# A hybrid decoder step on one core: scheduler priority for the attention's maxima and exponentials, other banks behind the decode's small products, and the closing steps moved

## The chip, the core and the metric

The program runs on one core of one Trainium2 chip. Five engines work side by side: TensorE (PE in the profile, its weight loads PEld), VectorE (DVE), ScalarE (ACT), GpSimd (POOL) and SyncE (SP). Each has a queue of its own, whose order the program fixes; SP and POOL issue most of the DMA transfers. TensorE's products go to PSUM, of which this kernel uses eight banks of 128 x 512 float32. The metric is device time in microseconds (us) of one launch; the verdict compares medians.

## The reference

One decoder layer is computed twice with the same weights: for a prompt of 1024 rows and for eight sample sequences with one new row each, which attend to 8192 cached positions in pages. Per layer: an input projection; eight heads of forgetting attention (softmax with a cumulated log gate) beside eight heads of spatial gating, both normalized and projected out; cross-attention to 256 memory tokens; a gated MLP with a short convolution. The part that this case touches is the attention of the prompt and the softmax of the samples:

```python
def fox_attend(q, k, v, cq, ck, qpos, kpos):
    s = jnp.einsum('bqhd,bkhd->bhqk', q, k).astype(jnp.float32) * (ATT_HEAD_DIM ** -0.5)
    s = s + (cq.astype(jnp.float32).transpose(0, 2, 1)[:, :, :, None]
             - ck.astype(jnp.float32).transpose(0, 2, 1)[:, :, None, :])
    s = jnp.where(kpos[None, :] <= qpos[:, None], s, -jnp.inf)
    p = jax.nn.softmax(s, axis=-1).astype(v.dtype)
    return jnp.einsum('bhqk,bkhd->bqhd', p, v)
```

```python
def merge_heads(att, sgu, g_att_out, g_sgu_out, w_o):
    return jnp.concatenate([rmsnorm(att, g_att_out), rmsnorm(sgu, g_sgu_out)], axis=-1) @ w_o
```

## The kernel before

**Two streams in one program.** `prompt()` (L1843) is a Python generator that traces the prompt's work: the input projections, the attention of the first 512 rows (`attention(0)`, mixed with the memory projections and the first half of the gating), the attention of the second 512 rows (`attention(1)`), and then, for each half, output projection, cross-attention and MLP. Each `yield t` states roughly how much work was traced. `sample()` is a second generator with the samples' work; a driver loop takes one step of it whenever the yields have added up to the pace of the phase (`PACE`, L76). So the samples' instructions lie between those of the prompt in program order.

**Who orders the queues.** A scheduler reads the traced program and fixes the order of each engine's queue when the program is built: among the instructions that are ready in its own model of time it takes the one with the highest priority, which is program order, earlier first. `tc.high_priority()` lifts the instructions of a block ahead of others that are ready. `tc.issue_after(x)` puts the block's instructions on the engine of `x` behind `x` in that queue; it adds an order and no wait. On the chip the order is fixed; each instruction waits only for its data and its buffers.

**The attention.** For each pair of heads (`hp`, four of them), each block of 256 rows (`blk`, two), each head `j` and each tile of 128 rows `ii`, `scores` (L795) writes one tile of scores with three matmuls per chunk (two where the chunk is off the diagonal): L807, L809 and, on the diagonal, the mask L811. In the first half a tile has one chunk in one bank `ba`; in the second it has two chunks in a pair of `ba` banks, of which there are two pairs. VectorE takes the negated maximum of each row (L813, L816), ScalarE the exponential with its row sums (L814, L817) into `p_`. `turn` (L829) transposes `p_` on TensorE (L836), up to four tiles of 128 x 128 per bank, and copies them to `u` or `t2` tiles on ScalarE (L843) or, for every fourth bank of the second half, on VectorE (L841). `values` (L845) multiplies with V (L852) and evicts (L861); `back` (L866) transposes the result (L872) and scales it (L874). `turn`, `values` and `back` go through a queue that lags two score tiles behind (`LA`). `setup` (L743) prepares the next pair of heads: transposes of q and k, copies, low parts (L774, L788) and loads (L759, L769 to L771).

**Banks.** `ba` has four banks, `bb` two, and one each is tagged `ms` and `dv`. The transposes, the values and the results of the attention take `bb`, and every third time `ms` (`B3`, L825, with `M3 = 3`). The memory projections and others take `ba`, and every third time `bb` (`BK`, L146).

**The decode of the samples.** For each of eight sequences and 16 steps, `kstep` (L1416) gathers 1 MB of cached K by an indirect DMA on the POOL queue (L1419) into one of four `kv` buffers; VectorE multiplies by q and sums. In the attention phases a step is cut into four pieces of a product (L1426) and a sum (L1427); elsewhere the pieces are larger (L1435, L1439). `vstep` (L1478) gathers V likewise (L1481) and TensorE multiplies it with the weights into `dv` (L1487). Between them stand three small products, each in the bank `ms` with one VectorE reader: `gates` (L1402: product L1409, read by L1411), `soft_all` (L1456: transpose L1459, read by L1462) and `soft_exp` (L1468: product L1472, read by L1474). `vmask` (L1498) reads `dv`.

**Closing a half.** `close` (L947) takes the squares of the attention's rows on ScalarE (`ssq_into`, L230), the reciprocal root, scales the rows in place on VectorE (L958) and stores them to DRAM (`an_d`, L960, on SP); it is a generator of three steps. In `prompt()` the first step of `close(0)`, the squares, is traced before `attention(1)`; `beside` (L963) then lets `attention(1)` run and takes one step of the closing after its yields number 0 and 2. The two first yields of `attention(1)`, which set up its first pair of heads, have been taken earlier, so number 0 is the one after its first tile of scores. `merge_in` (L981) reads the stored rows back. `lastexp` holds the exponential that was traced last.

Of the kernel before, what the change touches and what calls it, by code (L numbers as in the profile page):

```python
# [78 lines left out]
def build(nc, tc, ctx, a, phases=None):  # L79
# [61 lines left out]
    def BB():  # L141
        return psum.tile([P, 512], F32, tag="bb", bufs=2 + MB, name=nm("bb"))
# [8 lines left out]

    def MS():
        return BB() if MB else psum.tile([P, 512], F32, tag="ms", bufs=1, name=nm("ms"))

    def DV():
        return psum.tile([P, 512], F32, tag="dv", bufs=1, name=nm("dv"))
# [569 lines left out]
    def attention(hf, late=None, at=3):  # L726
# [68 lines left out]
        def scores(qkv, ls, blk, j, ii):  # L795

            qab, ka, kb, _ = qkv
            i = blk * 2 + ii
            e = (hf * 4 + i + 1) * P
            nch = 1 if e <= 512 else 2  # L800
            n = e // nch
            p_ = (WRAW(e) if PW else U([P, e])) if hf else T2(e)
            mx = sm([P, 1], "mx", 4)
            both = BA2().rearrange("p (c n) -> p c n", c=2)[:, :, :n] if nch == 2 else BA()[:, :n].unsqueeze(1)
            for ch in range(nch):
                s = both[:, ch, :]
                mmul(s, qab[j][:, 0, i * P : (i + 1) * P], ka[j][:, ch * n : ch * n + n], start=True, stop=False)  # L807
                diag = ch == nch - 1
                mmul(s, qab[j][0:68, 1, i * P : (i + 1) * P], kb[j][0:68, ch * n : ch * n + n], start=False, stop=not diag)  # L809
                if diag:  # L810
                    mmul(s[:, n - P :], ident_b, cmask_b, start=False, stop=True)  # L811
            if nch == 1:
                nc.vector.tensor_reduce(mx, s, axis=AX.X, op=ALU.max, negate=True)  # L813
                nc.scalar.activation(p_[:, :e], s, AF.Exp, bias=mx, accum_out=ls[:, ii, j : j + 1])  # L814
            else:
                nc.vector.tensor_reduce(mx, both, axis=AX.XY, op=ALU.max, negate=True)  # L816
                nc.scalar.activation(  # L817
                    p_[:, :e].rearrange("p (c n) -> p c n", c=2), both, AF.Exp, bias=mx, accum_out=ls[:, ii, j : j + 1]
                )
            lastexp[:] = [newest(ENG.Activation)]  # L820
            return p_

# [1 line left out]

        def B3():  # L825
            turns[1] += 1
            return MS() if turns[1] % M3 == M3 - 1 else BB()

        def turn(p_, pts, n, ii):  # L829

# [116 lines left out]
    def close(hf, att):  # L947

        ssa = sm([P, 4], "ssa", 1)
        for i in range(4):  # L950
            ssq_into(ssa[:, i : i + 1], att[i // 2][:, i % 2, :])
        yield
        r = rstd_of(ssa, AW, 4, "ra")
        yield
        for b2 in range(2):
            for i in range(2):
                t = att[b2][:, i, :]
                nc.vector.tensor_scalar(t, t, r[:, b2 * 2 + i : b2 * 2 + i + 1], None, op0=ALU.mult)  # L958
            t0 = hf * 4 + b2 * 2
            nc.sync.dma_start(an_d[t0 * P : (t0 + 2) * P, :].rearrange("(c p) d -> p c d", p=P), att[b2])  # L960
        yield
# [403 lines left out]
    def decode():  # L1365
# [36 lines left out]
        def gates(b, A):  # L1402
# [1 line left out]
            nc.vector.tensor_tensor(  # L1404
                tot, A.rearrange("p (h k) -> p h k", k=64)[:, :, 63], lfz[:, b * 8 : b * 8 + 8], op=ALU.add
            )
            ps = MS()
            with behind(ENG.PE):
                mmul(ps[:, :8], suf, tot, start=True, stop=True)  # L1409
            dt_ = dec("dec").rearrange("p (k h) -> p k h", h=8)  # L1410
# [43 lines left out]
            return pm  # L1454

        def soft_all(b, pm):  # L1456
            ps = MS()
            with behind(ENG.PE):
                nc.tensor.transpose(ps[:8, :P], pm, ident)  # L1459
            with tc.high_priority():  # L1460
# [6 lines left out]

        def soft_exp(b, st, dg):  # L1468
            s = st[1]
            ps = MS()  # L1470
            with behind(ENG.PE):
                mmul(ps[:, :8], ones, dg, start=True, stop=True)  # L1472
            with tc.high_priority():
# [369 lines left out]
    def prompt():  # L1843
# [24 lines left out]
        if LT > 3:  # L1868
            yield next(att1)
        ending = close(0, att)  # L1870
        next(ending)
        phase[0] = "att1"
        ba_pool(True)
        if G0R:
            att = yield from mix(gating(0), att1, 1 / G0R)
        else:
            att = yield from beside(att1, ending, (0, 2))
        ba_pool(False)
        ending = close(1, att)
        next(ending)  # L1880
# [143 lines left out]
```

## Time and profile before

| | |
|---|---|
| median of 3 runs | 1807.73 us (1807.55 to 1808.47) |
| profiled execution, its time | 1812.65 us |
| profiled execution, span from first to last instruction | 1810.9 us |
| mean granted TensorE clock of it | 0.987 |
| first attention half, beside the memory projections | about 262 to 374 us |
| second attention half | about 374 to 503 us |
| output projection and cross-attention, first half | about 503 to 724 us |
| first MLP | about 724 to 1098 us |

The profile shows one execution. Busy time counts an engine's instructions and no register, branch, semaphore or DMA-issuing ones; matmuls are pipelined, so their durations overlap. A wait is named by the instruction that waited and the one whose end released it. The granted clock is the share of the full TensorE clock that was passed in a stretch. A row of a timeline gives start, duration, engine, line, operation, output <- inputs, shapes and count, and in brackets the idle time of the engine before it with its releaser.

### The profile page before, as it was taken

The numbers are of one execution on the slowest core, as the hardware profiler recorded it, in microseconds if no ns is written. First come the engines' busy times: TensorE is split into PE (matmuls) and PEld (weight loads), VectorE is DVE, ScalarE is ACT, GpSimd is POOL, SyncE is SP. The second block draws the span as 40 slices with busy tenths as digits, with TensorE's granted clock in tenths as the row PEclk, the third lists the DMA queues.
The fourth block names the chain that finished last, engine by engine and source line by source line (L and its number), as shares of the span: only waits on it lengthen the run. The fifth ranks groups of instructions, "written<-read, shape, count | busy, mean of one in ns | idle before, by whom it ended". The sixth has DMA issues, their size and how long they took to land.

```text
span 1810.9 us, 25097 instructions
## 1 busy us (share of the span) xinstructions
PE 1741.1 (96%) x9637; PEld 1295.4 (72%) x9637; DVE 1398.3 (77%) x1729; ACT 735.3 (41%) x1378; POOL 503.7 (28%) x461
## 2 busy tenths in 40 slices
PE   8999999878999899999999999999989999999997
PEld 5887776656677667777777777766676678767775
DVE  4689668987788887999999899888875549855344
ACT  6332265465633544433323244235353323232332
POOL 1252333522133323233232132433322111001110
PEclk9999999988999999999999999999999999999999
DMA  8886889786596876689788788979878677568982
GB/s 300 305 296 228 303 303 341 251 276 195 214 403 259 344 306 269 261 285 342 298 293 320 291 310 309 382 286 361 315 273 318 241 278 263 182 262 292 360 313 82
DMA packets 157074, 521.06 MB, mean 288 GB/s; under 512 B 20874, under 2 KB 40842, under 8 KB 124186
## 3 DMA queue, kind: packets, MB, share of 16 engines
q0 software_dynamic: 57168, 341.14, 49.7%
q1 hardware_dynamic: 92874, 165.73, 26.5%
q10 hardware_dynamic: 6912, 12.59, 1.8%
q8 instruction: 76, 1.25, 0.3%
q14 instruction: 44, 0.36, 0.1%
HBM read 495.47 MB, written 23.93 MB: 287 GB/s over the span
## 4 chain that ended last, share of the span: by engine, by line
PE 50%; issue 8%; DMA 8%; DVE 7%; POOL 2%; ACT 1%; POOLq 0%; DVEq 0%; ACTq 0%
PE ba L272 6%; PE ba L274 6%; PE ba L273 6%; DMA kv<-cache_v,io 6%; PE dv L1487 3%; PE bb L272 3%; PE bb L273 3%; PE bb L274 3%; DVE s L1439 1%; DVE kv L1435 1%; DVE wl L236 1%; PE dv L331 1%; DMA kv<-cache_k,io 1%; PE dv L1763 1%; POOL kv L1419 1%
## 5 line engine op out<-in xcount | busy, mean ns | idle before, releaser
L235 ACT ACTIVATE wh<-wr 128x1024 fp32r<-128x1024 f32 (+2 forms) x220 | 228.2, 1043 | 451.2 <-PE ba L273 143.2
L236 DVE TENSOR_TENSOR wl<-wr,wh 128x1024 fp32r<-128x1024 f32 (+2 forms) x220 | 263.1, 1202 | 173.8 <-PE ba L274 57.1
L1419 POOL DMA_INDIRECT kv<-cache_k,io x128 | 196.7, 1537 | 578.5 <-DVE s L1439 323.1
L1435 DVE TENSOR_TENSOR kv<-kv,d 128x1024 f32<-128x1024 f32 (+1 forms) x156 | 258.1, 1682 | 32.6 <-DMA kv<-cache_k,io 27.3
L1439 DVE TENSOR_REDUCE s<-kv 128x16 f32<-128x1024 f32 (+1 forms) x156 | 258.6, 1676 | 0.0
L1481 POOL DMA_INDIRECT kv<-cache_v,io x128 | 167.6, 1310 | 258.7 <-PE dv L1487 179.9
L273 PE MATMUL ba<-u,wh 128*128 128x512 f32 x528 | 208.5, 395 | 2.4 <-DVE u L239 2.4
L272 PE MATMUL ba<-u,wh 128*128 128x512 f32 x528 | 209.5, 397 | 0.0
L274 PE MATMUL ba<-u,wl 128*128 128x512 f32 x528 | 209.1, 396 | 0.0
L272 PE MATMUL ba<-wh,u 128*128 128x512 f32 (+1 forms) x495 | 186.1, 379 | 0.9 <-ACT u L235 0.9
L273 PE MATMUL ba<-wl,u 128*128 128x512 f32 (+1 forms) x495 | 185.2, 375 | 1.3 <-DVE wl L236 1.3
L274 PE MATMUL ba<-wh,u 128*128 128x512 f32 (+1 forms) x495 | 183.4, 375 | 0.0
L1487 PE MATMUL dv<-kv,s 128*32 128x512 f32 x1024 | 123.9, 598 | 4.8 <-DMA kv<-cache_v,io 4.8
L274 PEld LDWEIGHTS ba<-u,wl 128*128 128x128 f32 x528 | 99.2, 188 | 29.1 <-issue 5.7
L273 PEld LDWEIGHTS ba<-u,wh 128*128 128x128 f32 x528 | 99.3, 188 | 27.0 <-DVE u L239 2.6
L272 PEld LDWEIGHTS ba<-u,wh 128*128 128x128 f32 x528 | 99.5, 189 | 25.7 <-issue 4.0
L272 PEld LDWEIGHTS ba<-wh,u 128*128 128x128 f32 x495 | 93.0, 188 | 25.0 <-issue 6.5
L272 PE MATMUL bb<-u,wh 128*128 128x512 f32 x272 | 108.5, 399 | 0.0
L273 PE MATMUL bb<-u,wh 128*128 128x512 f32 x272 | 108.0, 397 | 0.0
L274 PE MATMUL bb<-u,wl 128*128 128x512 f32 x272 | 107.9, 397 | 0.0
L273 PEld LDWEIGHTS ba<-wl,u 128*128 128x128 f32 x495 | 93.0, 188 | 20.3 <-DVE wl L236 2.1
L274 PEld LDWEIGHTS ba<-wh,u 128*128 128x128 f32 x495 | 92.9, 188 | 19.4 <-issue 1.6
(444 smaller groups left out, 3330.5 us busy)
## 6 DMA issues: line engine op xcount, KB each, us to landing
wr<-w_up SPq DMA_DIRECT2D x88, 512.0 KB
kv<-w_up POOLq DMA_DIRECT2D x22, 1024.0 KB
wr<-w_down SPq DMA_DIRECT2D x40, 512.0 KB
kv<-w_down POOLq DMA_DIRECT2D x11, 1024.0 KB
wr<-w_in SPq DMA_DIRECT2D x16, 512.0 KB
wr<-w_o SPq DMA_DIRECT2D x16, 512.0 KB
wr<-w_cq SPq DMA_DIRECT2D x16, 512.0 KB
wr<-w_co SPq DMA_DIRECT2D x16, 512.0 KB
```

Of the source, the lines that this page charges most:

```text
L235: nc.scalar.activation(h, src, AF.Copy)
L236: nc.vector.tensor_tensor(l, src, h.bitcast(F32), op=ALU.subtract)
L272: mmul(out, sh, mh, start=(i == 0), stop=False)
L273: mmul(out, sh, ml, start=False, stop=False)
L274: mmul(out, sl, mh, start=False, stop=(i == n - 1))
L331: mmul(ps[32 * j : 32 * j + 32, :w], xT[:, k, :] if nk == 8 else xT[:, k * 8 : k * 8 + 32], raw[:, q, j * w : (j + 1) * w], start=(k == 0) ...
L1419: nc.gpsimd.indirect_dma_start(kv, None, a["cache_k"], off(kidx[:, b, ch : ch + 1]))
L1435: nc.vector.tensor_tensor(kvv[:, i : i + m, :], kvv[:, i : i + m, :], qb.unsqueeze(1).broadcast_to((P, m, 512)), op=ALU.mult)
L1439: nc.vector.tensor_reduce(s[:, ch * 4 + i : ch * 4 + i + m, :].rearrange("p k h -> p (k h)"), kvv[:, i : i + m, :].rearrange("p k (h d) -> ...
L1481: nc.gpsimd.indirect_dma_start(kv, None, a["cache_v"], off(kidx[:, b, ch : ch + 1]))
L1487: mmul(dv[32 * j : 32 * j + 32, :], s[:, ch * 4 : ch * 4 + 4, :].rearrange("p k h -> p (k h)"), kvv[:, j, :], start=(ch == 1), stop=(ch == ...
L1763: mmul(ps[32 * j : 32 * j + 32, :P], xsT[:, k, :], rvs[j // 2][:, k, j % 2, :], start=(k == 0), stop=(k == 7), tile_position=(0, 32 * j),)
```

## The change

Four edits. A new function `MSD` gives the same `ms` bank as `MS` and sets a counter to 2; the three small products of the decode use it. `B3`, at the turns at which it would give `ms`, looks at the counter: while it is above 0 it counts down and gives `bb`. The maximum and the exponential of `scores` are traced under `tc.high_priority()`. The squares of `close` are queued behind the exponential that was traced last. And the first step of `close(0)` isn't taken before `attention(1)` but at the yield number 0 within it, the second at number 2 and the third at number 4, so that the squares follow the first tile of scores, the reciprocal root the third, and scaling and store the first half of the next pair's set-up, which comes after the fourth.

```diff
+    small_ = [0]
+
+    def MSD():
+        small_[0] = 2
+        return MS()
...
-            if nch == 1:
-                nc.vector.tensor_reduce(mx, s, axis=AX.X, op=ALU.max, negate=True)
-                nc.scalar.activation(p_[:, :e], s, AF.Exp, bias=mx, accum_out=ls[:, ii, j : j + 1])
-            else:
-                nc.vector.tensor_reduce(mx, both, axis=AX.XY, op=ALU.max, negate=True)
-                nc.scalar.activation(
-                    p_[:, :e].rearrange("p (c n) -> p c n", c=2), both, AF.Exp, bias=mx, accum_out=ls[:, ii, j : j + 1]
-                )
+            with tc.high_priority():
+                if nch == 1:
+                    nc.vector.tensor_reduce(mx, s, axis=AX.X, op=ALU.max, negate=True)
+                    nc.scalar.activation(p_[:, :e], s, AF.Exp, bias=mx, accum_out=ls[:, ii, j : j + 1])
+                else:
+                    nc.vector.tensor_reduce(mx, both, axis=AX.XY, op=ALU.max, negate=True)
+                    nc.scalar.activation(
+                        p_[:, :e].rearrange("p (c n) -> p c n", c=2), both, AF.Exp, bias=mx, accum_out=ls[:, ii, j : j + 1]
+                    )
...
         def B3():
             turns[1] += 1
-            return MS() if turns[1] % M3 == M3 - 1 else BB()
+            if turns[1] % M3 == M3 - 1:
+                if not small_[0]:
+                    return MS()
+                small_[0] -= 1
+            return BB()
...
     def close(hf, att):
 
         ssa = sm([P, 4], "ssa", 1)
-        for i in range(4):
-            ssq_into(ssa[:, i : i + 1], att[i // 2][:, i % 2, :])
+        with tc.issue_after(lastexp[0]):
+            for i in range(4):
+                ssq_into(ssa[:, i : i + 1], att[i // 2][:, i % 2, :])
...
         def gates(b, A):
-            ps = MS()
+            ps = MSD()
...
         def soft_all(b, pm):
-            ps = MS()
+            ps = MSD()
...
         def soft_exp(b, st, dg):
-            ps = MS()
+            ps = MSD()
...
         ending = close(0, att)
-        next(ending)
         phase[0] = "att1"
         ba_pool(True)
         if G0R:
             att = yield from mix(gating(0), att1, 1 / G0R)
         else:
-            att = yield from beside(att1, ending, (0, 2))
+            att = yield from beside(att1, ending, (0, 2, 4))
```

## The prediction

> **What bounds the kernel now.** I read the page first, then busy time by stage, then what TensorE waited for in the two attention stages, then single instructions around its longest waits.
>
> ```profile
> span 1810.9 us, 25097 instructions
> PE 1741.1 (96%) x9637; PEld 1295.4 (72%) x9637; DVE 1398.3 (77%) x1729; ACT 735.3 (41%) x1378; POOL 503.7 (28%) x461
> ```
>
> The span is 1810.9 us and TensorE is busy for 1741.1 of it: it sets the end, and 69.8 us of idle time are all that reordering can win, besides time lost to a slower clock. Where they lie (columns: stretch, its length, busy time of PE, PEld, DVE, ACT, POOL with counts, granted clock, DMA share, GB/s):
>
> ```profile
> 262.00:374.00 112.00, 101.79 (x599) 75.04 (x598) 94.55 (x177) 65.48 (x159) 44.87 (x60) 0.97 0.84 293
> 374.00:503.00 129.00, 114.37 (x770) 79.26 (x770) 101.88 (x167) 76.05 (x154) 33.27 (x44) 0.93 0.68 222
> 724.00:1098.00 374.00, 372.97 (x1758) 277.71 (x1757) 353.80 (x323) 134.25 (x204) 108.77 (x79) 1.00 0.80 300
> ```
>
> The first two rows are the prompt's attentions, first and second half: 10.2 and 14.6 us idle, and with a clock below 1. The third row, the first half of the gated MLP, has no gap (372.97 of 374): time won before 503 us reaches the end unless DMA takes it back.
>
> What TensorE waited for, first half and then second half of the attention (line waiting, releaser, total us, times, longest):
>
> ```profile
> PE ms L852 <- DVE dec L1411: 2.7, 1, 2.7
> PE bb L872 <- ACT t L861: 2.6, 4, 1.1
> PE bb L836 <- ACT t L814: 2.0, 2, 1.5
> PE ms L852 <- DVE s L1474: 1.2, 1, 1.2
> PE ms L852 <- DVE m L1462: 0.4, 1, 0.4
> ```
> ```profile
> PE ba L807 <- ACT wr L817: 5.8, 5, 1.9
> PE bb L836 <- ACT wr L817: 2.8, 3, 1.5
> PE ms L836 <- ACT wr L817: 2.0, 2, 1.2
> ```
>
> Two causes carry the idle time: the bank `ms`, held by a small decode product until VectorE has read it (2.7 + 1.2 + 0.4 = 4.3 us), and exponentials that come late (2.0 us in the first half, 5.8 + 2.8 + 2.0 = 10.6 in the second; 12.6 in all, over 12 waits). The 2.6 us on L861 are an eviction the change doesn't touch.
>
> **Why an exponential is late.** Timelines of TensorE, VectorE and ScalarE around 398 us:
>
> ```profile
> 396.80 0.23 PE L811 MATMUL ba<-cmask_b,ident_b 128*128 128x128 bf16 x1
> ...
> 401.46 0.98 PE L836 MATMUL bb<-cp,wr 128*128 128x128 f32 x7 [1.51 <-ACT wr L817]
> ```
> ```profile
> 396.35 0.67 DVE L1427 TENSOR_REDUCE s<-kv 128x8 f32<-128x512 f32 x1
> 396.94 0.68 DVE L1501 TENSOR_TENSOR d<-dv,cp 128x512 f32<-128x512 f32 x1
> 397.54 0.48 DVE L874 TENSOR_TENSOR u<-bb,rl 128x128 f32<-128x128 f32 x2
> 397.93 1.28 DVE L1426 TENSOR_TENSOR kv<-kv,d 128x512 f32<-128x512 f32 x2
> 399.13 1.08 DVE L816 TENSOR_REDUCE mx<-ba 128x1 f32<-128x896 f32 x1
> ```
>
> The scores end at 396.80 + 0.23 = 397.03. Their maximum starts at 399.13, 2.10 us later: vmask (L1501), two scalings (L874) and two decode pieces (L1426) went first. The exponential follows, and TensorE stands 1.51 us. This is what the priority aims at.
>
> **The price of a gap in clock.** Stretches before and inside slots of half clock (columns as above):
>
> ```profile
> 352.60:356.10 3.50, 3.26 (x17) 3.27 (x17) 3.44 (x9) 2.48 (x8) 2.20 (x3) 0.51 0.72 202
> 366.30:369.70 3.40, 1.65 (x14) 0.84 (x11) 3.34 (x7) 1.99 (x6) 0.00 (x0) 1.00 1.00 396
> 369.70:373.10 3.40, 3.38 (x15) 3.28 (x16) 1.79 (x5) 2.90 (x8) 0.00 (x0) 0.50 1.01 401
> 380.00:383.40 3.40, 3.40 (x16) 2.89 (x15) 3.40 (x8) 2.20 (x6) 2.17 (x3) 0.50 0.03 5
> 400.40:403.80 3.40, 1.66 (x12) 1.41 (x12) 3.40 (x5) 2.60 (x5) 0.00 (x0) 1.00 1.02 422
> 403.80:407.20 3.40, 2.86 (x12) 2.74 (x12) 3.40 (x8) 1.97 (x5) 0.00 (x0) 0.51 0.95 388
> 427.70:431.10 3.40, 1.55 (x9) 0.93 (x8) 3.40 (x7) 1.21 (x2) 0.00 (x0) 1.00 1.20 245
> 431.10:441.40 10.30, 9.00 (x37) 7.05 (x35) 8.04 (x13) 5.13 (x10) 1.55 (x2) 0.50 0.59 197
> 441.40:503.00 61.60, 58.63 (x428) 40.13 (x428) 43.93 (x71) 37.98 (x76) 12.91 (x16) 1.00 0.61 215
> ```
>
> After a slot in which TensorE was busy for 1.55 to 1.66 of 3.4 us, the next slot runs at half clock. The five such stretches hold 3.26 + 3.38 + 3.40 + 2.86 + 9.00 = 21.9 us of busy time, half of which, 10.95, is lost.
>
> **The change, term by term** (against the profiled execution's 1812.65 us).
>
> A, other banks. After each small decode product the next two turns that would take `ms` take `bb`. The three waits of 4.3 us have no other cause than that product; what replaces them is `bb`, two buffers that also serve every third product elsewhere. Bounds: 4.3 won; 2.6 lost, if the one `bb` wait listed for L872 doubles. The first is nearer, because it is these very rows; the replacement is not free, so I take 2.5 won.
>
> B, priority. Of the 2.10 us ahead of the maximum above, only the piece already running (0.68 at most) would remain, and the gap of 1.51 closes. A mean wait on an exponential is 12.6 / 12 = 1.05 us, less than the 1.4 thus removed; but not every late maximum has decode pieces ahead of it, and some waits have another cause, as at the start of the second half:
>
> ```profile
> 378.11 0.63 ACT L230 ACTIVATE junk<-u 128x512 bf16<-128x512 f32 x1
> ...
> 378.74 0.78 ACT L817 ACTIVATE wr<-ba,mx 128x640 f32<-128x640 f32 x1
> ```
>
> There the closing squares (L230) hold the first exponential until 378.74. Queuing them behind an exponential wins 378.74 − 378.11 = 0.63 us once, at most. Bounds for B with the squares: 0 and 12.6. I take half, 6, since some of it must reappear as the next link of scores, maximum, exponential, transposes.
>
> C, clock. The slots at 369.7, 403.8 and 431.1 follow a stretch with one of these waits; they hold 3.38 + 2.86 + 9.00 = 15.2 us, half of it 7.6. A gap that only shrinks may leave the slot slow. Bounds 0 and 10.95, and 3.4 / 2 = 1.7 lost for each new slow slot; I take 4 won.
>
> By the Trainium skill, "TensorE: Matmul & The Clock Gate", section on HAM oscillation, the clock falls after idle gaps of more than about 3.4 us; the longest wait here is 1.9 us, so by it C would be 0 and the sum 4 us worse. The rows disagree: slots with scattered waits of 1 to 2 us were enough. The same page's Part 4 says that transposes don't count as activity, which would keep the clock low whatever gaps close; the last row, full of transposes, ran 61.6 us at 1.00, and speaks against that.
>
> D, what is paid. Decode pieces move behind the maxima; no instruction is added. What hides it is VectorE's idle time, 129 − 101.88 = 27.1 us in the second half. Later pieces free their K buffers later, the gathers on the POOL queue issue later, and TensorE's products with V may wait:
>
> ```profile
> PE dv L1487 <- DMA kv<-cache_v,io: 4.8, 4, 1.9
> ```
>
> That is 4.8 us in the whole execution; I take a quarter more, 1 us (bounds 0 and 4.8). The closing steps move too: their scaling and store are traced after the fourth score and the first half of the next heads' set-up, instead of after the third score, so that set-up's loads (L769) come ahead of the store on SP, which takes its queue in order:
>
> ```profile
> 383.67 1.16 SPq L960 DMA_DIRECT2D an_d<-u  x2
> ...
> 385.94 1.61 SPq L769 DMA_DIRECT2D u<-ks_d  x2
> ```
> ```profile
> L981 SPq DMA_DIRECT2D u<-an_d x4: 370/395/421, 458.3 to 1108.5; - x4
> ```
>
> The stored rows are first read back at 458.3, 74 us later, so the data is in time. But the two `u` tiles that are stored stay taken for about one score more, 129 / 32 = 4.0 us, and the next heads' tiles or the transposed exponentials want them. Bounds 0 and 4.0; I take 1.5, nearer to nothing, since the set-up is needed only four scores (16 us) after it is traced.
>
> Sum: 2.5 + 6 + 4 − 1 − 1.5 = 10 us. 1812.65 − 10 = 1802.65 for a profiled execution. The median of the runs shown, 1807.73, lies 4.92 below the profiled 1812.65, so I forecast 1797.7. With gains of A to C between a third and one and a half of what I take (4.2 to 18.8) and 0 to 5 paid, this forecast's own range is 1789 to 1809 (its part above 1804 is counted under R2).
>
> **Rivals.**
>
> R1, slower: VectorE takes its queue in order, and a maximum placed ahead of decode work waits there with everything behind it if its scores aren't finished. Place: the start of the second half.
>
> ```profile
> 374.00:441.40 67.40, 55.74 (x343) 39.13 (x342) 57.94 (x97) 38.07 (x78) 20.37 (x28) 0.87 0.74 228
> ```
> ```profile
> DVE mx L816 <- PE ba L811: 12.7, 8, 4.0
> ```
>
> VectorE has 67.4 − 57.94 = 9.5 us free there for some 17 maxima: from 0.56 us of added standing per maximum on, the stage grows. At 1 us each it is 17 − 9.5 = 7.5 longer, and one more slow slot 1.7: 1807.73 + 9.2 = 1817. For it: maxima already stood 12.7 us for scores. Against it: in the same stage it is TensorE that waits for maxima.
>
> R2, no change: each closed wait opens the next. Scores have two pairs of `ba` banks, so TensorE can't run ahead further than two; a sooner exponential meets an eviction (L861, 2.6 us in four waits) or the next maximum. Gains of A and B halve to 4.2, C and the prices cancel: within 3.6 us of the median, 1806. Also here: the order, fixed when the program is built, hardly changes.
>
> R3, slower: the `u` tiles held longer keep the transposed exponentials, and so the banks, waiting (D's 4.0 us), `bb` collides (2.6) and V comes late (4.8): 11.4 paid, and of the gains only B's 6 stays: 5.4 slower, 1813. It decides once the three prices pass the gains that are left. Against it: each alone is small.
>
> R4, faster by less: the clock doesn't follow these gaps, C is 0: 1801.7. For it speaks the slow stretch from 431.1, which lasted although TensorE was busy for 9.00 of 10.3 us in it. It is what the Trainium skill's section on HAM oscillation in "TensorE: Matmul & The Clock Gate" would give.
>
> **How the numbers follow.** Forecast 0.40, R4 0.15, R2 0.12, R1 0.22, R3 0.11: the rows show the removed waits directly, while R1 and R3 rest on waits that aren't there yet. About 0.2%, 3.6 us, is what a measurement of this kernel can tell from no change: faster 0.55, same 0.12, slower 0.33. For the range I leave out half of the forecast's better tail and of R1's worse one: 1788 to 1817.
>
> **What would show it.** A right: no wait of L852 on L1411, L1474 or L1462. B right: waits of L807 and L836 on L817 fall from 10.6 to about 5 us, and no decode piece stands between the last score and its maximum but a running one. C right: the clock of the second half rises above 0.95. D: waits of L1487 on V under 6 us, and the second head's scores not later than before. I am wrong if the idle time of TensorE before 503 us falls by less than 4 us, or if it falls and the stages behind 503 us grow by as much.

## The result, and the profile after

The changed kernel takes 1826.0 us (median of 6 runs, 1819.1 to 1829.3) where the kernel before takes 1808.1 (6 runs): ratio 1.0098, 95% interval 1.0083 to 1.0112. It is 18 us slower, and outside the range that was given. Measured again later, beside other kernels, it took 1823.9 against 1808.8, ratio 1.0078 (1.0061 to 1.0095). The profiled execution took 1819.07 us. It is the fastest of the six, and only 6.4 us longer than the profiled execution of the kernel before (1812.65), so the two profiles show about a third of the 18 us. The head of its page:

```profile
span 1817.2 us, 25091 instructions
PE 1739.7 (96%) x9637; PEld 1291.3 (71%) x9637; DVE 1399.6 (77%) x1729; ACT 733.9 (40%) x1378; POOL 504.8 (28%) x461
```

Its lines are a little further down in the file: L813, L815 and L817 are the scores (L807 to L811 before), L820 and L823 the maxima, L821 and L824 the exponentials, L847 the transposes, L854 their evictions (L843), L863 the values (L852) with the eviction L872, L883 `back`, L970 the closing scalings (L958), L241 the split of a weight on ScalarE (L235), L1438 and L1439 the decode pieces.

Busy time of the two attention halves, each from its own first score to the next stage's mark (second half's first score, last score). Before:

```profile
261.60:371.60 110.00, 99.79 (x593) 73.54 (x591) 94.89 (x177) 64.12 (x157) 44.87 (x60) 0.98 0.83 291
371.60:482.50 110.90, 96.93 (x634) 68.26 (x633) 88.57 (x147) 65.31 (x135) 28.59 (x39) 0.92 0.66 212
```

After:

```profile
261.80:382.30 120.50, 103.32 (x599) 73.15 (x597) 93.81 (x175) 65.00 (x157) 44.98 (x60) 0.96 0.77 263
382.30:492.10 109.80, 95.35 (x627) 66.72 (x626) 90.76 (x149) 63.48 (x133) 29.07 (x39) 0.92 0.67 216
```

In the profiles the loss arises in the first half: 10.5 us longer, with 120.50 − 103.32 = 17.2 us of idle TensorE instead of 10.2. The second half, which the prediction was mostly about, is 1.1 us shorter, its idle time 14.5 instead of 14.0 and its clock the same. What TensorE waits for, first half and then second half:

```profile
PE ms L863 <- ACT u L854: 6.7, 2, 6.0
PE bb L847 <- ACT t L821: 4.1, 2, 3.2
PE bb L883 <- ACT t L872: 2.0, 3, 1.2
```
```profile
PE ba L813 <- ACT wr L824: 9.1, 6, 4.1
PE ms L847 <- ACT wr L824: 1.8, 2, 0.9
PE bb L847 <- ACT wr L824: 1.3, 2, 0.8
```

The three waits of the values on a small decode product are gone, as meant. In their place stand one of 6.0 us on an eviction and one of 3.2 on an exponential, and the second half's exponentials hold TensorE for 12.2 us instead of 10.6. The longest, on ScalarE and TensorE of the changed kernel:

```profile
292.24 0.69 ACT L726 ACTIVATE t<-ba,rm 128x512 f32<-128x512 f32 x1 [0.34 <-PE ba L280]
299.03 1.06 ACT L241 ACTIVATE wh<-wr 128x1024 fp32r<-128x1024 f32 x1 [6.11 <-DMA wr<-w_cv]
299.99 0.58 ACT L854 ACTIVATE u<-ms 128x512 f32<-128x512 f32 x1
300.47 0.48 ACT L854 ACTIVATE u<-bb 128x384 f32<-128x384 f32 x1
```
```profile
294.41 0.23 PE L817 MATMUL ba<-cmask_b,ident_b 128*128 128x128 bf16 x1
300.62 1.12 PE L863 MATMUL ms<-u,u 128*64 128x256 f32 x2 [5.98 <-ACT u L854]
```

The two evictions need only transposes that ended by 293.9, but ScalarE takes its queue in order, and ahead of them stands the split of a tile of `w_cv`, which waits 6.11 us for its load. In the kernel before the same split stands at the same place of ScalarE's queue (only an exponential, now behind the evictions, stood ahead of them), and doesn't wait:

```profile
293.06 1.06 ACT L235 ACTIVATE wh<-wr 128x1024 fp32r<-128x1024 f32 x1
294.03 0.68 ACT L814 ACTIVATE t<-ba,mx 128x512 f32<-128x512 f32 x1
294.69 0.60 ACT L843 ACTIVATE u<-ms 128x512 f32<-128x512 f32 x1
```

What is different is the load. The queues of GpSimd and SyncE, and the DMA share of two stretches, before:

```profile
288.82 1.47 POOL L1419 DMA_INDIRECT kv<-cache_k,io  x1 [2.70 <-DVE mx L813]
290.60 0.97 POOL L1419 DMA_INDIRECT kv<-cache_k,io  x1 [0.30 <-DVE wl L236]
```
```profile
289.45 5.61 SPq L249 DMA_DIRECT2D wr<-w_cv  x4
```
```profile
288.00:290.00 2.00, 2.00 (x10) 1.65 (x9) 2.00 (x3) 1.85 (x4) 1.18 (x1) 1.00 0.70 276
290.00:292.00 2.00, 2.00 (x10) 1.62 (x9) 0.89 (x2) 2.00 (x5) 1.26 (x2) 1.00 0.58 206
```

After:

```profile
287.31 1.01 POOL L1431 DMA_INDIRECT kv<-cache_k,io  x1 [0.30 <-DVE mx L820]
288.62 1.29 POOL L1431 DMA_INDIRECT kv<-cache_k,io  x1 [0.30 <-issue]
```
```profile
289.15 4.53 SPq L255 DMA_DIRECT2D wr<-w_cv  x4
```
```profile
288.00:290.00 2.00, 2.00 (x11) 1.62 (x10) 1.79 (x2) 1.93 (x4) 1.61 (x2) 1.00 1.02 335
296.00:298.00 2.00, 0.00 (x0) 0.00 (x0) 0.00 (x0) 0.00 (x0) 0.00 (x0) 0.85 1.01 399
```

The loads are issued at the same time (289.45 and 289.15). Before, one gather of K went ahead of the first of them, the DMA engines had room (0.70 and 0.58), and the split ran 3.6 us after the issue. Now two gathers of 1 MB each are ahead, the engines are full, and the tile lands 9.9 us after its issue; from 296 to 298 us none of the core's computing engines is busy. That the gathers make the difference is read from timelines; no run changed them alone. But all sixteen profiles of this study agree: in the eight with at most one gather just ahead of the load the split starts 3.6 to 5.1 us after the load's issue, in the eight with two 8.8 to 11.6 us after it.

### The profile page after: what moved, and what is told of

Read it like the earlier page. It is cut to its first block, busy times and chain, and to the rows that moved or that the text cites. A ratio compares the mean times of both kernels' runs of the same rounds, so it can differ in the third digit from the quotient of the medians.

```text
span 1817.2 us, 25091 instructions
## 1 busy us (share of the span) xinstructions
PE 1739.7 (96%) x9637; PEld 1291.3 (71%) x9637; DVE 1399.6 (77%) x1729; ACT 733.9 (40%) x1378; POOL 504.8 (28%) x461
## 4 chain that ended last, share of the span: by engine, by line
PE 51%; DMA 8%; issue 7%; DVE 5%; POOL 2%; ACT 2%; POOLq 0%; DVEq 0%
PE ba L278 6%; PE ba L280 6%; PE ba L279 6%; DMA kv<-cache_v,io 6%; PE dv L1499 4%; PE bb L278 3%; PE bb L279 3%; PE bb L280 3%; DVE kv L1447 1%; PE dv L337 1%; PE ba L1076 1%; PE ba L1078 1%; PE ba L1077 1%; PE dv L1775 1%; PE ba L1096 1%
## 5 line engine op out<-in xcount | busy, mean ns | idle before, releaser
L241 ACT ACTIVATE wh<-wr 128x1024 fp32r<-128x1024 f32 (+2 forms) x220 | 228.4, 1043 | 459.4 <-PE ba L279 143.3
L1493 POOL DMA_INDIRECT kv<-cache_v,io x128 | 166.6, 1302 | 260.7 <-PE dv L1499 186.1
L279 PE MATMUL bb<-u,wh 128*128 128x512 f32 x272 | 107.9, 397 | 0.0
```

The lines of the kernel that those rows point to most:

```text
L241: nc.scalar.activation(h, src, AF.Copy)
L279: mmul(out, sh, ml, start=False, stop=False)
L1493: nc.gpsimd.indirect_dma_start(kv, None, a["cache_v"], off(kidx[:, b, ch : ch + 1]))
```

## The experiments

### The four edits, one by one

Four kernels take the change apart. The first has the priority alone:

```diff
+            with tc.high_priority():
                 if nch == 1:
                     nc.vector.tensor_reduce(mx, s, axis=AX.X, op=ALU.max, negate=True)
...
```

> Only the priority of maxima and exponentials is added to the kernel before; the other three edits are left out. Theory N (the priority has no effect: with it the program is built with the same order on all five queues as before): ratio 1.000, within 0.2%, and the idle time of TensorE between 262 and 503 us as before, 24.8 us within 2. Rival P (it is the priority that costs the changed kernel its 18 us, as maxima that stand at VectorE's head): ratio 1.008 to 1.011.

Measured: 1806.8 us against 1810.2, ratio 0.9979 (0.9963 to 0.9995). In the profiles all instructions of TensorE, VectorE, ScalarE and GpSimd (9637, 1729, 1378 and 461) and all transfers of SyncE come in the same order as before, one for one. So this ratio is one of two equal programs, and shows what the measurement can't tell: 0.2%. Theory N holds. The priority was the largest term of the prediction.

The second has the other banks alone (`small_`, `MSD`, `B3`), the third the closing edits alone:

```diff
-        for i in range(4):
-            ssq_into(ssa[:, i : i + 1], att[i // 2][:, i % 2, :])
+        with tc.issue_after(lastexp[0]):
+            for i in range(4):
+                ssq_into(ssa[:, i : i + 1], att[i // 2][:, i % 2, :])
...
-        next(ending)
...
-            att = yield from beside(att1, ending, (0, 2))
+            att = yield from beside(att1, ending, (0, 2, 4))
```

> Only the other banks are added to the kernel before: MSD at the three small products of the decode, and the counter in B3. Theory B (the loss of 18 us, ratio 1.0098, comes from the other banks alone, which reorder the first attention half: first score of the second half about 10 us later than before): ratio 1.008 to 1.011, second half's first score 8 to 12 us later than in the kernel before. Rival C (it comes from the closing steps): ratio 0.997 to 1.002. Rival S (they share it, or only both together do it): 1.003 to 1.006.

> Only the closing steps are changed in the kernel before: the squares behind the last traced exponential, and the three steps at numbers 0, 2 and 4. Theory B (the other banks carry the loss): ratio 0.998 to 1.002, and the first half of the attention, which is traced ahead of them, as before (second half's first score within 2 us). Rival C (the closing steps carry it): 1.006 to 1.011, lost between 374 and 503 us. Rival S (they share it): 1.003 to 1.006.

Measured: banks alone 1.0019 (1.0006 to 1.0032), the second half's first score at 381.7 us as in the changed kernel; closing alone 0.9991 (0.9979 to 1.0003), first score at 372.3. The 10 us of the first half are the banks' (Theory B), but most of it comes back later, and the ratio is the one that Rival C gave; that of the closing edits is the one that Theory B gave. So neither carries the loss alone, and both ratios lie within the 0.2%.

The fourth is the change without the priority.

> The changed kernel without the priority of maxima and exponentials; the other three edits stay. Theory N (the priority has no effect): ratio 1.008 to 1.011 against the kernel before, as the changed kernel, with the same stage times within 3 us. Rival P (the priority carries the loss): 0.997 to 1.002. If the priority wins something that the other edits hide: above 1.012.

Measured: 1824.0 us, 1.0080 (1.0059 to 1.0100). Its order is that of the changed kernel but for two maxima on VectorE, each of which the priority puts ahead of one instruction of the decode. One of the two places, without the priority and with it:

```profile
408.20 1.01 DVE L1521 TENSOR_REDUCE vsum<-d 128x64 f32<-128x512 f32 x1
409.13 1.08 DVE L822 TENSOR_REDUCE mx<-ba 128x1 f32<-128x896 f32 x1
```
```profile
409.24 1.08 DVE L823 TENSOR_REDUCE mx<-ba 128x1 f32<-128x896 f32 x1
410.23 1.04 DVE L1522 TENSOR_REDUCE vsum<-d 128x64 f32<-128x512 f32 x1
```

So beside the other edits the priority isn't quite without effect on the order, but the time shows nothing of it (1.0080 without, 1.0098 and 1.0078 with it). Theory N's ratio came; of its stage times one, from the last score to the second half's output projection, misses the 3 us: 652.3 against 647.8 us.

So 0.19% and −0.09% alone become 0.8 to 1% together. The two edits that do something don't add up, and the rest of the study is about that.

### The split at ScalarE's head

One instruction is moved in the changed kernel, the split that waits; it stands five places later on ScalarE, behind a store, the two evictions and two exponentials, and nothing else on any queue has moved:

```diff
-                with tc.issue_after(before):
-                    ws = [wload(wpair(w, kk, n * 512, 512), 1024, ahead.pop(0) if ahead else None) for kk in range(4)]
+                ws = []
+                for kk in range(4):
+                    late_ = w is a["w_cv"] and n == 1 and kk == 0
+                    raw = ahead.pop(0) if ahead else wraw(wpair(w, kk, n * 512, 512), 1024)
+                    with tc.issue_after(exps[-6] if late_ else before):
+                        ws.append(wload(wpair(w, kk, n * 512, 512), 1024, raw))
...
+            exps.append(lastexp[0])
...
```

> The changed kernel with one instruction moved: on ScalarE's queue the split of the fifth w_cv tile (L241), which stood for 6.11 us on its DMA, goes behind the two evictions and two exponentials that follow it there; every other place in every queue stays. Theory H (TensorE's 5.98 us at 294 us are that split standing at ScalarE's head, and the half-clock slot behind it is its consequence): no wait of TensorE over 1.5 us between 290 and 305 us, the second half's first score at 373 to 377 us instead of 382.3, and ratio 1.003 to 1.007 against the kernel before, where the changed kernel has 1.0098. Rival D (VectorE's half of the same split, or the memory projection's products that need it, stand next): the gap moves, first score after 380 us, ratio 1.008 to 1.011.

ScalarE in this run:

```profile
293.67 0.60 ACT L859 ACTIVATE u<-ms 128x512 f32<-128x512 f32 x1 [0.51 <-PE ms L852]
294.19 0.49 ACT L859 ACTIVATE u<-bb 128x384 f32<-128x384 f32 x1
...
300.23 1.06 ACT L241 ACTIVATE wh<-wr 128x1024 fp32r<-128x1024 f32 x1 [4.53 <-DMA wr<-w_cv]
```

The load is as late as before, and the split still stands 4.53 us, but nothing that TensorE needs is behind it: TensorE has no listed wait between 285 and 310 us, and the second half's first score comes at 374.5. Theory H holds in its three numbers; ratio 1.0062 (1.0042 to 1.0082). The same move with the other banks alone:

> The other banks alone (as in the second run of this study), with the one split of w_cv moved behind two evictions and two exponentials on ScalarE's queue. Theory H (that split's place is what the leftover turns cost): second half's first score at 373 to 377 us instead of 381.7, and since the second half itself was 3 us shorter with the other banks alone, ratio 0.996 to 0.999. Rival W (what is won before 503 us is lost again in the stages behind): first score as early, but ratio 1.000 to 1.003, as without the move.

Measured: 0.9990 (0.9978 to 1.0002), first score at 375.3; without the move it was 1.0019. So this one place costs 6 to 8 us by the end of the first half (381.7 to 375.3 here, 382.3 to 374.5 above) and some 5 us at the end.

Why the order changes there, at 294 us, when the attention's first small product comes at 313, is the next run: the counter of `MSD` is set to 0 where the attention begins.

```diff
         phase[0] = "att0"
+        small_[0] = 0
```

> The changed kernel with the counter of MSD set to 0 where the first attention half begins, so that the two turns left over from the small product at 193 us no longer take bb in the attention; the three small products inside the first half keep their other banks. Theory L (the leftover is what reorders ScalarE's queue ahead of 313 us, and with it comes the gap of 5.98 us): no such gap, second heads' pair and third (hp2) within 2 us of the kernel before, ratio 1.001 to 1.006. Rival M (the turns moved behind the small products at 313, 338 and 366 us cost as much): third pair's first score still 5 us later, ratio 1.007 or more.

Measured: 1.0019 (1.0005 to 1.0032); the longest wait between 285 and 310 us is 2.0 us, on an exponential, and the third pair's scores start at 329.8 us, 2.2 later than before, where the changed kernel has 334.3. That is Theory L but for 0.2 us: two turns left over from a product at 193 us, long read by then, are the first that take `bb` in the attention, and with them comes the order that puts the gathers ahead.

> The kernel before with the other banks alone and the counter set to 0 where the attention begins: what term A of the prediction priced. Theory A (the three waits of 4.3 us close and little takes their place): ratio 0.9965 to 0.999, none of these three waits left. Rival M (the turns that move cost more than the waits): 1.001 to 1.004.

This is what term A priced. Measured: 1.0026 (1.0013 to 1.0040), Rival M's number. But its first half,

```profile
261.80:372.90 111.10, 102.67 (x598) 74.51 (x597) 94.05 (x176) 64.95 (x159) 44.52 (x60) 0.97 0.82 288
```

has 111.10 − 102.67 = 8.4 us of idle TensorE instead of 10.2, the three waits are gone, and the last score of the second half came at 478.5, 4.0 us earlier than before. The gain was there and was lost behind 1131 us, in the stage that the end of this part looks at.

### What late maxima cost

> The kernel before with the samples' decode held back for the second attention half (its pace there so long that it falls into the stages behind): VectorE has no decode pieces between 374 and 503 us. The time as a whole says nothing, as the held pieces are done later. Theory V (exponentials are late because decode pieces go ahead of the maxima on VectorE): TensorE's waits on L817 in the second half fall from 10.6 to under 3 us and the half gets 8 us shorter or more, clock above 0.96. Rival K (each closed wait opens the next: evictions, set-up, banks): waits on L817 still over 6 us, or other waits in their place, the half at most 4 us shorter.

The edit is `'att1': 11.0` to `1000.0` in `PACE`. This kernel ran once, under the profiler. The second half from its first to its last score, and its waits:

```profile
370.90:469.10 98.20, 87.85 (x585) 63.99 (x584) 52.15 (x87) 64.60 (x137) 14.72 (x25) 0.95 0.32 97
```
```profile
PE ba L807 <- ACT wr L817: 6.0, 5, 1.9
...
PE ms L836 <- ACT wr L817: 0.3, 1, 0.3
```

Between the two theories: the half is 12.7 us shorter (V), but waits on exponentials are still 6.3 of 10.6 us (K, just), with VectorE free for 46 of 98 us, and TensorE's wait on the set-up (L788) grew from 0.8 to 2.6. Most of the 12.7 is TensorE's own work (96.93 to 87.85 us busy: 49 matmuls fewer and a better clock). So the decode's work ahead of maxima accounts for 4.3 us of late exponentials there, all of it taken together.

### What the closing edits do beside the other banks

With the split out of the way, the two kernels differ by the closing edits alone, and by 13 us (1.0062 and 0.9990). Their second halves, first the other banks alone, then with the closing edits, then the changed kernel itself in its second profile:

> The changed kernel itself, to have it beside the others on one chip, and a second profile of it. Ratio 1.008 to 1.011. Theory C (the part of the loss that the first profile doesn't show lies in slots of half clock in the second attention half): second half's clock below 0.92, first half as in the first profile within 2 us. Rival X (it lies in the second half's cross-attention, about 1205 to 1360 us): clock of the second half 0.93 or more, and that stage over 3 us longer than in the first profile.

```profile
375.30:481.30 106.00, 91.61 (x628) 63.59 (x626) 89.35 (x149) 63.75 (x133) 29.42 (x39) 0.97 0.68 224
```
```profile
374.50:488.90 114.40, 100.75 (x629) 71.24 (x628) 90.79 (x150) 64.20 (x133) 28.88 (x39) 0.87 0.63 208
```
```profile
381.30:491.20 109.90, 95.36 (x628) 66.61 (x626) 90.71 (x149) 63.58 (x133) 29.05 (x39) 0.92 0.65 217
```

Idle time is the same in all (14.4, 13.7, 14.5 us), and so is the work; the clock makes the difference. But the last two have the same order on every queue of this half, so the 4.5 us between them don't come from the order. Three profiles whose queues there are those of the kernel before (itself, with the priority, with another pace of a later stage) took 110.9, 112.3 and 114.8 us; two with the other banks alone 106.0 and 107.9; four with the closing edits beside them (the two changed ones, without the priority, with the split behind) 109.8 to 114.4. So the other banks shorten this half and the closing edits lengthen it again, but by how much can't be told from one profile each. Of the second profile neither theory had it all: the clock was 0.92, as in the first, and the cross-attention's stretch 3.2 us longer (230.5 and 227.3). What the closing edits change there, on VectorE of that second profile:

```profile
394.03 2.32 DVE L970 TENSOR_SCALAR u<-u,rar 128x512 f32<-128x512 f32 x4
...
404.33 0.69 DVE L1513 TENSOR_TENSOR d<-dv,cp 128x512 f32<-128x512 f32 x1
404.94 0.48 DVE L885 TENSOR_TENSOR u<-bb,rl 128x128 f32<-128x128 f32 x2
405.33 1.28 DVE L1438 TENSOR_TENSOR kv<-kv,d 128x512 f32<-128x512 f32 x2
406.53 1.22 DVE L823 TENSOR_REDUCE mx<-ba 128x1 f32<-128x1024 f32 x1
```

The four scalings now stand behind the fourth maximum, with the set-up behind them, and the sixth maximum, which the other banks alone have ahead of vmask (L1513), goes behind it, two scalings of `back` and three decode pieces; ScalarE has nothing to do for 5.5 us and TensorE stands 4.1. With the closing edits alone this wait is there too, 4.7 us, at the time of the kernel before (0.9991). Two runs take this apart, both with the split moved. One keeps everything else and puts the scalings behind the eighth maximum; the other keeps the squares at their old place and pins only the scalings behind the fourth (its numbers are `(0, 3)`):

```diff
-                nc.vector.tensor_scalar(t, t, r[:, b2 * 2 + i : b2 * 2 + i + 1], None, op0=ALU.mult)
+                with tc.issue_after(lastmax[0]) if hf == 0 else nullcontext():
+                    nc.vector.tensor_scalar(t, t, r[:, b2 * 2 + i : b2 * 2 + i + 1], None, op0=ALU.mult)
...
-            att = yield from beside(att1, ending, (0, 2, 4))
+            att = yield from beside(att1, ending, (0, 2, 9))
```

> The changed kernel with the w_cv split moved as before, and the closing's four scalings (L970) put on VectorE behind the eighth maximum of the second half instead of behind the fourth, so that they no longer go ahead of the first set-up's subtractions; with it the order puts the sixth and seventh maximum ahead of decode pieces that stood before them. Theory S (it is the late scalings among set-up, vmask and decode pieces that make TensorE's 4.1 us wait and the slow clock behind it, and so the 13 us between the runs with and without the closing edits): no wait of TensorE on L824 over 2.5 us, second half 108 us or shorter, ratio 0.997 to 1.002. Rival Q (the squares behind the first exponential cost it, wherever the scalings are): ratio 1.004 to 1.007, second half 109 us or longer.

> The other banks with the w_cv split moved, the squares where they were before (ahead of the first exponential), and only the four scalings pinned behind the fourth maximum, as they stand in the changed kernel. Theory S: a wait of TensorE of 3 us or more around 400 us, second half 109 us or longer, ratio 1.003 to 1.007. Rival Q: second half 108 us or shorter, ratio 0.997 to 1.001.

TensorE's waits on the second half's exponentials, scalings later and then scalings late alone:

```profile
PE ba L817 <- ACT wr L828: 6.7, 6, 2.1
```
```profile
PE ba L817 <- ACT wr L827: 9.4, 5, 4.6
```

Measured, scalings later: longest such wait 2.1 us, second half 105.9 us, ratio 1.0034 (1.0021 to 1.0047), between the two theories. Scalings late alone: a wait of 4.63 us, second half 108.5 us, between the two, yet ratio 0.9989 (0.9973 to 1.0005), Rival Q's number. So the place of the scalings makes the wait, both ways. What the wait is worth stays open: without it the ratio goes from 1.0062 to 1.0034 (5 us, and the intervals overlap a little), with it from 0.9990 to 0.9989, and the closing edits alone carry it at no cost. It is not the 13 us; the rest has another home.

### The cross-attention of the second half

From the first product of the second half's output projection to its first MLP product, by kernel; the last column is the wait of the decode's products with V on their gather between 1225 and 1300 us:

| kernel | ratio | second attention half, us, clock | that stretch, us | wait on V, us |
|---|---|---|---|---|
| before | | 110.9, 0.92 | 229.3 | 1.6 |
| priority only (order of before) | 0.9979 | 112.3, 0.91 | 225.9 | 1.4 |
| closing only | 0.9991 | 110.6, 0.94 | 223.7 | 1.0 |
| changed, first and second profile | 1.0098, 1.0078 | 109.8, 0.92; 109.9, 0.92 | 227.3; 230.5 | 2.6; 3.9 |
| changed without priority | 1.0080 | 111.5, 0.89 | 227.9 | 2.8 |
| changed, counter reset | 1.0019 | 112.1, 0.91 | 224.7 | 1.4 |
| changed, split behind | 1.0062 | 114.4, 0.87 | 234.0 | 1.3 |
| the same, scalings later | 1.0034 | 105.9, 0.95 | 229.4 | 3.2 |
| banks, counter reset | 1.0026 | 105.6, 0.95 | 232.0 | 3.5 |
| banks only | 1.0019 | 107.9, 0.94 | 225.3 | none |
| banks, split behind | 0.9990 | 106.0, 0.97 | 227.0 | none |
| the same, scalings late | 0.9989 | 108.5, 0.92 | 221.3 | none |

The last three have a wait on V nowhere in that stretch, all others have one. These three also share an order in the cross-attention that none of the others has: of VectorE's 227 instructions there, 66 stand at another place than before, in the others at most 24. By this order the kernels fall into groups, each with one order on VectorE, ScalarE and GpSimd. The order of the kernel before (itself, priority only, changed with the counter reset) took 224.7 to 229.3 us; that of the changed kernel (it twice, without priority, split behind, scalings later, and the banks with the counter reset, whose gain was lost here) 227.3 to 234.0; that of the last three 221.3 to 227.0. The edit touches only banks of the attention; how it reaches an order 850 us later (the two `bb` buffers taken in another turn from then on, perhaps) was not tested. GpSimd's queue with the other banks and the split behind, then in the changed kernel (V's gathers are L1496 and L1493):

```profile
1242.32 0.94 POOL L1434 DMA_INDIRECT kv<-cache_k,io  x1 [7.92 <-DVE cr L1205]
1247.21 1.56 POOL L1496 DMA_INDIRECT kv<-cache_v,io  x1 [3.95 <-PE dv L1502]
1249.07 0.94 POOL L1496 DMA_INDIRECT kv<-cache_v,io  x1 [0.30 <-issue]
```
```profile
1244.92 0.94 POOL L1431 DMA_INDIRECT kv<-cache_k,io  x1 [5.25 <-DVE s L1451]
1253.90 0.94 POOL L1431 DMA_INDIRECT kv<-cache_k,io  x1 [8.04 <-DVE s L1451]
1255.14 0.95 POOL L1493 DMA_INDIRECT kv<-cache_v,io  x1 [0.31 <-issue]
```

In the second, a gather of K that waits 8.04 us for VectorE stands ahead of V's, and the products with V wait 3.9 us. But counted from the stretch's first product (1131.8 and 1139.4), V's gather goes out after 115.4 and 115.7 us and these products start after 127.0 and 127.3: in the first TensorE has other work until then. So the wait marks the order and isn't by itself what it costs. The banks alone, then, lose 10 us in the first attention half and win some in the second; the closing edits take that gain away and bring an order of the cross-attention whose stretches are 5.7 us longer on the mean (230.2 against 224.5). No run changed this order alone. At equal attention halves (scalings later, 1.0034, and banks with the split behind, 0.9990) it would have to be worth 8 us, of which the two profiles show 2.6 (spans of 1810.9 and 1808.3), so this part of the cause is argued and not shown.

Two runs asked whether a thinner decode in that stretch (`'mid1': 8.0`) lets the banks' 4 us through:

> The kernel before with one number changed: the samples' pace beside the second half's output projection and cross-attention 8.0 instead of 6.8, so that about a seventh of the decode steps there falls into the second MLP. Alone it says nothing of the change (0.99 to 1.01); it is the base for the next run.

> The other banks with the counter reset, and the pace 8.0: to be read against the run with the pace alone. Theory W (the 4 us that the other banks win by 482 us are lost where decode work and the second half's cross-attention crowd VectorE at 1230 to 1290 us): with the thinner decode there the gain passes, 3 to 5 us faster than the run with the pace alone. Rival E (the banks cost in the stages behind in another way, or the stage's length differs from execution to execution): as slow against it as against the kernel before, 2 to 5 us slower.

Measured: 1.0044 (1.0026 to 1.0062) with the pace alone, 1.0030 (1.0015 to 1.0045) with banks and reset. The second is 2.4 us faster where it was 4 us slower, which leans to W, but the intervals overlap and it stays open. No version of this study is measurably faster than the kernel before; the one interval below 1 is that of the priority alone, the same program.

## Why the prediction was wrong

The first step that failed is term B, "Bounds for B with the squares: 0 and 12.6. I take half, 6": the priority was to put the maxima ahead of the decode pieces, but the order is fixed when the program is built, and it comes out the same with the priority alone; beside the other edits two maxima move by one place. The pieces that stand ahead of a late maximum were traced ahead of it; the likely reason that the planner puts them there is that in its own time the scores aren't finished yet, which was argued and not tested. R2's last sentence had this possibility, for all edits together, and it got too small a share. And 6 was probably too much: with no decode piece left, 4.3 us of the waits went.

B is 6 of the 28 us between the forecast, 10 won, and the measurement, 18 lost. The other step that failed is the sum itself, "2.5 + 6 + 4 − 1 − 1.5": it adds terms that were each priced in the order of the kernel before. Alone the edits measured nothing (the priority, the same order), some 3 us lost (the banks, 1.0019) and 1.5 won (the closing, 0.9991); together they lost 14 to 18, and the 12 to 16 us between are in no term.

Term A, 2.5 won: the mechanism was right, its price was not. The three waits closed in every kernel with the other banks, and by themselves brought the last score 4.0 us forward. The lower bound, 2.6 lost, counted only other waits on `bb`. It left out that a bank chosen otherwise re-orders the queues, and that the counter outlives the product: the turns left over from 193 us reach the attention. That let a standing split hold two evictions and cost 6 to 8 us by the end of the half.

Term C, 4 won: its sign was wrong in the first half, where half clock sets in within the new gap of 5.98 us and outlasts it (0.50 from 298 to 304 us; the half's clock is 0.96 and 0.97 in the two profiles, 0.98 before), and it is 0 in the second (0.92 each time). Three profiles with the order of the kernel before had 0.92, 0.91 and 0.88 there, so a gain of this size could hardly have been read from one profile. Two readings under C were off: the longest wait in the lists is 2.7 us and not 1.9, which is the second half's, and the row called full of transposes has 154 of them among its 428 matmuls, so it tells little about transposes.

Term D, 2.5 paid: alone the closing edits cost nothing (0.9991), beside the banks about 13 us. V late and held-up tiles were named, and TensorE's waits on V came to 5.5 and 7.6 us in the two profiles instead of 4.8, but the longest is 750 us further on, in an order of the cross-attention that no term had priced. What wasn't priced either is the four scalings' own place on VectorE, among set-up and decode pieces, with a new wait of 4.1 us behind them. The squares behind the first exponential won about the 0.63 us given as the most: before, it starts 378.74 − (377.37 + 0.82) = 0.55 us after its maximum has ended, in the second profile of the changed kernel 386.15 − (385.31 + 0.81) = 0.03.

R1 came closest in time (1817), but not by its mechanism: the second half's maxima wait on their scores no longer than before (12.7 us, in eight waits):

```profile
DVE mx L823 <- PE ba L817: 11.9, 7, 3.7
```

R3 named V late and colliding banks, with a price of 5.4 us; the split that holds two evictions and the scalings' place aren't in it. R2's own sum gives 1807.7 − 4.2 = 1803.5, not its 1806. Of the signs listed, the idle time before 503 us was to fall by 4 us; in the two halves it rose from 10.2 + 14.0 to 17.2 + 14.5 us. The second half's waits on late exponentials were to fall to about 5 us; they rose to 12.2.

What the stages don't show: the kernel before took 1812.65 us when it was profiled, 3.9 above its median of 1808.8, so differences of profiles (6.4 us for the first profile of the changed kernel, 1823.03 − 1812.65 = 10.4 for the second) are smaller than those of medians (18 and 15 us). Which stage of a typical execution of the kernel before is shorter than in its profile stays open, and with it the last 5 us of the run with the scalings later, whose profile has the same span as that of the kernel before, 1810.9 us.

## What to carry to other kernels

Before a scheduling hint is priced, build the program with it alone and compare the order of the queues: a hint that moves no instruction is worth nothing, and one that moves some far from its place must be priced where they land. Look in every in-order queue for instructions that wait for a DMA, and for what stands behind them; here a load that came some 10 us late cost TensorE nothing once two short evictions no longer stood behind its first reader. Profile the same order more than once before reading a few microseconds out of one stage: equal queues gave halves of 109.8 to 114.4 us. And read an edit's effect stage by stage, then run the edits alone and together: here 0.2% and nothing made 0.8 to 1%, because edits that reorder queues don't add up.

## What was not expected of the hardware

A load of 512 KB that a split reads was there 3.6 us after its issue at the latest in the kernel before and took 9.9 us in the changed one, with one gather of 1 MB just ahead of it or two; over all profiles it was 3.6 to 5.1 us at the latest with at most one, 8.8 to 11.6 at the latest with two.

With the decode in it, the clock of the second attention half was 0.87 to 0.97 at nearly the same idle time, 13.3 to 14.9 us, none of it in one piece of more than 4.7 us. Kernels with the same queues there differed too: 0.92, 0.92 and 0.87 (changed kernel twice, with the split behind), and 0.92, 0.91 and 0.88 (kernel before, with the priority, with another pace of a later stage). The Trainium skill, "TensorE: Matmul & The Clock Gate", section on the second HAM failure mode (psum-queue depth-cycling), says that brief and frequent idling between groups of matmuls is enough to make the clock swing. These rows agree as far as they go: the sum of the idle time doesn't tell the clock. What does was not tested.
